# An mLSTM step with the state of a head pair in one block of 128 partitions, GpSimd scaling the old state, and a reciprocal root of one third-order and one Newton step

## The chip, the core and the metric

The kernel runs on one core of a Trainium2 chip. A core has five engines, each with its own queue in program order: TensorE (PE in the profile; its weight loads are a row of their own, PEld), VectorE (DVE), ScalarE (ACT), GpSimd (POOL) and SyncE (SP, which issues DMAs here). PE writes to PSUM, which DVE and ACT read; everything else lies in SBUF. The metric is the device time of one execution in microseconds. The time before is 2581.78 us, the median of three runs between 2577.17 and 2588.86.

## What is computed

One inference step of a two-layer decoder trunk for 1024 new prompt tokens and 8 single-token samples: layer 0 mixes tokens with an mLSTM, layer 1 with multi-head latent attention, and a SwiGLU block follows each. The change lies in the mLSTM of the prompt and in the root that the norms share. The mLSTM runs over chunks of tokens (64 in the reference, 128 in the kernel; the result is the same recurrence). For each head it keeps a matrix state C (64 x 128) and a vector n (64):

```python
def step(carry, xs):
    C, n, m = carry
    ...
    s = jnp.einsum('bhtd,bhsd->bhts', qb, kb) * w_intra
    num = w_inter[..., None] * jnp.einsum('bhtd,bhde->bhte', qb, C) + jnp.einsum('bhts,bhse->bhte', s, vb)
    den = w_inter * jnp.einsum('bhtd,bhd->bht', qb, n) + jnp.sum(s, axis=-1)
    h = num / jnp.maximum(jnp.abs(den), jnp.exp(-m_t))[..., None]
    ...
    C_new = w_C[..., None, None] * C + jnp.einsum('bhs,bhsd,bhse->bhde', w_s, kb, vb)
    n_new = w_C[..., None] * n + jnp.einsum('bhs,bhsd->bhd', w_s, kb)
    return (C_new, n_new, m_new), h
...
h = h * lax.rsqrt(jnp.mean(h * h, axis=-1, keepdims=True) + EPS)
```

Every norm is a root of the form rsqrt(mean + EPS).

## The kernel before

Everything is fp32 in the mLSTM's own products; the large projections are split into a high and a low part and take three products each (`mm3`, L132 to L137). The eight heads lie in two groups of four (hg 0 and 1), and the 1024 tokens in eight chunks c of 128. So `mlstm` (L402) makes 16 steps, i = 2c + hg, in its loop from L500 on. One step is `mlstm_chunk` (L639), in this order:

- E, the weights inside the chunk: DVE (L650) prepares them in the tile Gb, ACT takes the exponential (L651), PE makes k·q on 64 partitions (L656), DVE multiplies (L658).
- kt, the weighted keys (L664), and vn, the values with a column of ones (L666, L670), so that column 128 of a product is the normaliser.
- qw, the queries times the decay (POOL, L677), and wc, the decay at the chunk's end (POOL, L675).
- per pair of heads a PSUM bank: E·vn (L685) and, from chunk 1 on, qw·C added to it (L687). ACT takes |den| (dn, L688) and the sums of squares (ssq, L691).
- kt·vn for the new state (L697), two heads beside each other on 64 columns each, and four DVE operations (L703) that scale the old C and add it. In chunk 0 they are copies (L701).
- the denominators (dn, r: L713, L715), the norm (L716 to L720, with the root of L192) and hn, the normed output (L723, into the tile of E). Its transposes (L727) and the copy to v (L728) belong to the next step.

C is a tile of 128 partitions x 4 heads x 129 columns. A head's state fills only 64 of the partitions, those that its queries lie on in qw; the other 64 stay zero from a memset (L480), so that PE can run over all 128 rows.

The root (L192) makes a first guess with an integer shift and a subtraction (L198, L199) and then three Newton steps of three operations (L201 to L203). It is called once a step on 128 x 4, once for the samples on 128 x 64, six times on up to nine columns (`rms_tok`, L243), and once on 128 x 258 (`rs_of`, L228).

What runs beside a step: in steps 1 to 8 one tile of the output gate's projection (`proj_o`, L465; 72 matmuls of 344 columns) and the samples' own states; in steps 9 to 14 one tile of the output projection of the first 512 tokens (`op_tile`, L885: 24 matmuls of 512 columns, the residual added by DVE into x at L899, the squares summed by POOL at L905), the split of the next weights (wl, L118), and from step 12 on the gating of the other half (L488, L121). The order on each engine comes from a scheduler that works with estimated costs; a few places are fixed by `issue_after`. An engine takes its instructions strictly in that order.

Of the kernel before, what the change touches and what calls it, by code (L numbers as in the profile page):

```python
# [12 lines left out]
AF = mybir.ActivationFunctionType  # L13
ALU = mybir.AluOpType
# [4 lines left out]
P = 128  # L19
# [10 lines left out]
L = 128  # L30
# [61 lines left out]
class Kern:  # L92
# [99 lines left out]
    def rsqrt(self, pool, v, shape, tag, w=None):  # L192
        V = self.nc.vector
        y = self.t(pool, shape, tag + "y")
        u = self.t(pool, shape, tag + "u")
        if w:
            y, u = y[:, :w], u[:, :w]
        V.tensor_scalar(y.bitcast(I32), v.bitcast(I32), 1, None, op0=ALU.logical_shift_right)  # L198
        V.tensor_scalar(y.bitcast(I32), y.bitcast(I32), -1.0, float(0x5F3759DF), op0=ALU.mult, op1=ALU.add)  # L199
        for _ in range(3):  # L200
            V.scalar_tensor_tensor(u, y, -0.5, y, op0=ALU.mult, op1=ALU.mult)  # L201
            V.tensor_tensor(u, u, v, op=ALU.mult)
            V.scalar_tensor_tensor(y, u, 1.5, y, op0=ALU.add, op1=ALU.mult)  # L203
        return y

    def newton(self, y, u, v):
# [120 lines left out]
    def load_x(self):  # L327
# [74 lines left out]
    def mlstm(self, xz, rs, early):  # L402
        nc = self.nc
        w_in = self.mlstm_w_in[0]
        p1 = self.pool("m1")
        v = self.t(p1, [P, 8, T], "v")
# [52 lines left out]
        pi = self.pool("mi")  # L459
# [16 lines left out]

        self.C = []
        for hg in range(2):
            C = self.t(pi, [P, 4, 129], f"C{hg}")
            nc.gpsimd.memset(C, 0.0)  # L480
            self.C.append(C)
        def loaded(og, i, h, zs):
            nc.sync.dma_start(og, o_d[:, h, 512 * i + zs.start:512 * i + zs.stop])
            return og, i, h, zs
# [154 lines left out]
    def mlstm_chunk(self, pi, c, hg, q, k, v, Gb, wb):  # L639
        nc = self.nc  # L640
        V = nc.vector
        s = slice(c * L, (c + 1) * L)
        h4 = slice(hg * 4, hg * 4 + 4)
        j2 = slice(hg * 2, hg * 2 + 2)
# [7 lines left out]
        for hh in range(2):  # L652
            ps = self.mmt("sc")[:, :2 * L]
            for j in range(2):
                r = slice(hh * 64, hh * 64 + 64)
                nc.tensor.matmul(ps[:, j * L:(j + 1) * L], k[r, hg * 2 + j, s], q[r, hg * 2 + j, s], start=True, stop=True)  # L656
            e = E.rearrange("p (j r) t -> p r j t", r=2)[:, hh]
# [3 lines left out]
        ps = self.tp()  # L661
# [5 lines left out]
        ps = self.tp()  # L667
# [3 lines left out]
        C = self.C[hg]  # L671
        qw = None
        if c > 0:
            wc = self.t(pi, [P, 2], "wc", bufs=3)
            nc.gpsimd.tensor_copy(wc, wb[:, :, L - 1])  # L675
            qw = wb
            self.wc = nc.gpsimd.tensor_tensor(qw, q[:, j2, s], wb, op=ALU.mult)  # L677
        dn = self.t(pi, [P, 4], "dn", bufs=2)
        sq = self.t(pi, [P, 4], "ssq", bufs=2)
        banks = []  # L680
        for h0 in (0, 2):
            ps = self.mmt("sc")[:, :258].rearrange("p (j e) -> p j e", e=129)
            for j in range(2):
                h = h0 + j
                nc.tensor.matmul(ps[:, j], E[:, h], vn[:, h], start=True, stop=c == 0)  # L685
                if c > 0:
                    nc.tensor.matmul(ps[:, j], qw[:, h // 2], C[:, h], start=False, stop=True)  # L687
            nc.scalar.activation(dn[:, h0:h0 + 2], ps[:, :, 128], AF.Abs)  # L688
            for j in range(2):
                junk = self.t(pi, [P, L], "junk", bufs=1)  # L690
                nc.scalar.activation(junk, ps[:, j, 0:128], AF.Square, accum_out=sq[:, h0 + j:h0 + j + 1])  # L691
            banks.append((ps, h0))

        ps = self.tp()[:, :258].rearrange("p (j e) -> p j e", e=129)
        for h in range(4):
            r = slice((h % 2) * 64, (h % 2) * 64 + 64)
            nc.tensor.matmul(ps[r, h // 2], kt[:, h], vn[:, h], start=True, stop=True)  # L697
        for h in range(4):
            r = slice((h % 2) * 64, (h % 2) * 64 + 64)
            if c == 0:  # L700
                ins = V.tensor_copy(C[r, h], ps[r, h // 2])  # L701
            else:
                ins = V.scalar_tensor_tensor(C[r, h], C[r, h], wc[r, h // 2:h // 2 + 1], ps[r, h // 2], op0=ALU.mult, op1=ALU.add)  # L703
        self.pin = ins.ins
        if c == NCK - 1:
            for hh in range(2):
                r = slice(hh * 64, hh * 64 + 64)
                Cr = C.rearrange("p (hp hh) e -> p hh hp e", hh=2)[r, hh]
                nc.gpsimd.dma_start(self.C_p[0, 0].rearrange("(hp hh) d e -> hh d hp e", hh=2)[hh, :, j2], Cr[:, :, 0:128])
                with nc.allow_non_contiguous_dma(reason="512 values"):  # L710
                    nc.gpsimd.dma_start(self.n_p[0, 0].rearrange("(hp hh) (d e) -> hh d hp e", hh=2, e=1)[hh, :, j2], Cr[:, :, 128:129])

        V.tensor_tensor(dn, dn, em_t, op=ALU.max)  # L713
        r = self.t(pi, [P, 4], "r", bufs=2)
# [4 lines left out]
        y = self.rsqrt(pi, sq, [P, 4], "f")  # L719
        V.tensor_tensor(y, y, r, op=ALU.mult)  # L720
        hn = E
        for ps, h0 in banks:
            self.hn = V.tensor_tensor(hn[:, h0:h0 + 2], ps[:, :, 0:128], y[:, h0:h0 + 2].unsqueeze(2).to_broadcast([P, 2, L]), op=ALU.mult)  # L723
        yield
        ps = self.tp()
        for j in range(4):
# [1383 lines left out]
```

## Time and profile before

| | |
|---|---|
| median of three runs | 2581.78 us |
| the profiled execution, its own time | 2603.12 us |
| its span | 2601.3 us |
| granted clock of PE, mean | 0.983 |
| mLSTM steps 0 to 15 | about 204 to 455 us of the span |

The profile is of one execution, and its time is its own; it is not one of the three runs. Busy times of engines overlap. PE's rows are pipelined: a row lasts longer than the distance to the next row's start, so distances between starts tell more than lengths. In a row of a timeline stand start, length, engine, line, operation, output<-inputs, shapes and a count, and in brackets how long the engine sat idle and what ended it. In a row of one line's instructions stand the shortest, the median and the longest length in ns.

### The profile page before, as it was taken

To read this page: it belongs to the slowest core of one execution; us is meant where nothing else is said; L and a number is where in the kernel's file an instruction comes from. 1 tells how busy PE (TensorE), PEld (TensorE's weight loads), DVE (VectorE), ACT (ScalarE), POOL (GpSimd) and SP (SyncE) were. 2 spreads that over 40 slices of the span, in tenths; PEclk is the share of its full clock that TensorE was granted. 3 is DMA by queue.
4 is the path that set the end of the run, shared out by engine and by line. 5 is a ranking of instruction groups with operands and counts; after the bars stand their busy time and mean duration, and the time that the engine had idled before them with its cause. 6 is when DMAs were issued, how large, how long until landed. Compare 5 with 4: busy or idle time off the path is not lost.

```text
span 2601.3 us, 54299 instructions
## 1 busy us (share of the span) xinstructions
PE 2510.5 (97%) x21151; PEld 2367.6 (91%) x21151; DVE 1864.6 (72%) x4491; ACT 1328.5 (51%) x3282; POOL 606.3 (23%) x636
## 2 busy tenths in 40 slices
PE   8999999999999999999988889999999999999998
PEld 8999987999999999999976767767899999999998
DVE  4345678897777777666557877768498877777765
ACT  4122344465666666554354555656256656556543
POOL 1021222201111111122335545442211111111102
PEclk9999999999999999999988999999999999999999
DMA  6153554427666566654566676664535566665663
GB/s 196 41 83 95 147 138 106 157 78 149 121 129 124 115 122 128 122 163 150 192 226 247 237 259 225 210 242 147 191 106 113 119 129 127 130 127 115 122 137 113
DMA packets 332087, 382.35 MB, mean 147 GB/s; under 512 B 23433, under 2 KB 263054, under 8 KB 323510
## 3 DMA queue, kind: packets, MB, share of 16 engines
q0 software_dynamic: 60992, 186.65, 31.9%
q1 hardware_dynamic: 258838, 182.04, 23.3%
q10 hardware_dynamic: 12000, 10.20, 1.2%
q8 instruction: 166, 2.72, 0.4%
q14 instruction: 91, 0.75, 0.1%
HBM read 253.37 MB, written 125.44 MB: 146 GB/s over the span
## 4 chain that ended last, share of the span: by engine, by line
PE 69%; DVE 9%; DMA 4%; issue 4%; ACT 2%; POOL 1%; SPq 0%; another core or an unknown queue 0%; POOLq 0%; ACTq 0%; DVEq 0%
PE sc L136 12%; PE sc L134 12%; PE sc L135 12%; PE mm L136 5%; PE mm L135 5%; PE mm L134 5%; PE ss L1892 2%; PE ss L134 2%; PE ss L135 2%; PE ss L136 2%; DMA nat<-in_cache_latent_dram,idx 2%; PE ss L1921 2%; DVE tt L1885 2%; PE mm L1785 1%; DVE wl L118 1%
## 5 line engine op out<-in xcount | busy, mean ns | idle before, releaser
L1215 POOL DMA_DIRECT2D x_d<-wl x72 | 86.8, 1206 | 992.6 <-DVE wl L1214 357.1
L117 ACT ACTIVATE wh<-wr 128x512 fp32r<-128x512 f32 (+2 forms) x167 | 133.4, 799 | 199.7 <-PE mm L135 136.1
L1885 DVE STREAM_TRANSPOSE tt<-nat 128x1024 f32<-128x1024 f32 x128 | 155.4, 1228 | 28.6 <-DMA nat<-in_cache_latent_dram,idx 20.4
L1892 PE MATMUL ss<-tt,qbd 128*32 128x128 f32 x2560 | 101.7, 289 | 18.2 <-issue 8.3
L1892 PEld LDWEIGHTS ss<-tt,qbd 128*32 128x32 f32 x2560 | 76.9, 115 | 40.7 <-issue 17.7
L118 DVE TENSOR_TENSOR wl<-wr,wh 128x1024 fp32r<-128x1024 f32 (+2 forms) x80 | 92.8, 1161 | 28.2 <-ACT wh L117 27.0
L117 ACT ACTIVATE b<-u 128x256 fp32r<-128x256 f32 (+1 forms) x252 | 98.5, 414 | 20.4 <-PE ss L136 6.3
L118 DVE TENSOR_TENSOR b<-u,b 128x256 fp32r<-128x256 f32 (+1 forms) x252 | 103.1, 422 | 6.8 <-ACT b L117 5.4
L1215 POOL DMA_DIRECT2D x_d<-st x72 | 102.4, 1422 | 8.6 <-DVE dC L118 3.5
L134 PE MATMUL mm<-zh,wh 128*128 128x344 f32 x320 | 103.5, 323 | 0.0
L135 PE MATMUL mm<-zl,wh 128*128 128x344 f32 x320 | 103.4, 323 | 0.0
L136 PE MATMUL mm<-zh,wl 128*128 128x344 f32 x320 | 103.3, 323 | 0.0
L118 DVE TENSOR_TENSOR wh<-S,wh 128x512 fp32r<-128x512 f32 x108 | 74.5, 690 | 34.6 <-ACT wh L117 34.3
L117 ACT ACTIVATE wh<-S 128x512 fp32r<-128x512 f32 x108 | 67.9, 629 | 44.4 <-PE sc L136 32.1
L1742 ACT ACTIVATE wr<-sc,mx,rqt 128x512 f32<-128x512 f32 (+2 forms) x96 | 64.6, 676 | 39.5 <-DVE mx L1737 22.8
L134 PE MATMUL sc<-zh,wh 128*128 128x344 f32 x256 | 82.9, 325 | 0.2 <-DVE q L432 0.2
L1785 PE MATMUL mm<-wh,vt 128*128 128x256 f32 (+1 forms) x320 | 74.6, 298 | 8.5 <-ACT wh L117 6.3
L135 PE MATMUL sc<-zl,wh 128*128 128x344 f32 x256 | 82.1, 321 | 0.0
L136 PE MATMUL sc<-zh,wl 128*128 128x344 f32 x256 | 82.0, 320 | 0.0
L1878 POOL DMA_INDIRECT nrp<-in_cache_k_rope_dram,idx x64 | 61.5, 961 | 64.5 <-DVE tt L1885 30.2
L905 POOL TENSOR_TENSOR ss<-ss,sq 128x512 f32<-128x512 f32 (+2 forms) x36 | 51.2, 1423 | 99.4 <-ACT sq L904 99.3
L130 POOL TENSOR_TENSOR wl<-spl,wh 128x512 fp32r<-128x512 f32 x43 | 54.7, 1284 | 83.4 <-ACT spl L129 80.8
(1084 smaller groups left out, 10701.6 us busy)
## 6 DMA issues: line engine op xcount, KB each, us to landing
wr<-in_ffn_w_gate_up_dram SPq DMA_DIRECT2D x96, 512.0 KB
x_d<-st POOLq DMA_DIRECT2D x72, 520.0 KB
x_d<-wl POOLq DMA_DIRECT2D x72, 512.0 KB
dr<-in_ffn_w_down_dram SPq DMA_DIRECT2D x72, 256.0 KB
wr<-in_mlstm_w_in_dram SPq DMA_DIRECT2D x24, 512.0 KB
wr<-in_mlstm_w_out_dram SPq DMA_DIRECT2D x16, 512.0 KB
q<-qn_d SPq DMA_DIRECT2D x28, 256.0 KB
wr<-in_mla_w_o_dram SPq DMA_DIRECT2D x14, 512.0 KB
```

The source lines that it names most:

```text
L117: ins = nc.scalar.activation(hi, src, AF.Copy)
L118: self.low = e.tensor_tensor(lo, src, hi.bitcast(F32), op=ALU.subtract)
L130: nc.gpsimd.tensor_tensor(lo, x, hi.bitcast(F32), op=ALU.subtract)
L134: mm(ps, wh, xh, start=start, stop=False, **kw)
L135: mm(ps, wh, xl, start=False, stop=False, **kw)
L136: self.last = mm(ps, wl, xh, start=False, stop=stop, **kw)
L1215: nc.gpsimd.dma_start(self.x_d[:, 2 * dp:2 * dp + 2, 512 * i:512 * i + 2 * PW[i]], st[i], accum_op=ALU.add)
L1742: nc.scalar.activation(px[:, ks], o, AF.Exp, bias=mx[:, 0:1], scale=f, accum_out=sm[:, c:c + 1])
L1785: nc.tensor.matmul(o, x, y, start=i == 0, stop=i == len(ops) - 1)
L1878: nc.gpsimd.indirect_dma_start(out=nrp[:, s].rearrange("p s c -> p (s c)"), out_offset=None, in_=rop, in_offset=ix)
L1885: V.transpose(out=tt, in_=src.rearrange("p s (c i) -> p c s i", i=32))
L1892: nc.tensor.matmul(psS[32 * j:32 * j + 32, u * P:u * P + P], self.qbd[:, b, cb], tt[:, c, 4 * j:4 * j + 4].rearrange("p s k -> p (s k)"), ...
```

## The change

- C becomes 128 partitions x 2 pairs x 129: the state of an even head lies on partitions 0 to 63, that of the odd head of the same pair on 64 to 127. There are no zeros in it, and no memset.
- qw·C takes only the 64 partitions of its head. The two PSUM banks of a step now hold the even and the odd heads, so both products of a bank take the same half.
- kt·vn already lay in that form, so the new state is one DVE addition of 128 x 258 (a copy in chunk 0). The old state is scaled before by POOL into a new tile Cw (two buffers), which replaces the copy wc.
- The root has one third-order step and one Newton step, seven operations in place of nine behind the first guess.

```diff
-        for _ in range(3):
-            V.scalar_tensor_tensor(u, y, -0.5, y, op0=ALU.mult, op1=ALU.mult)
-            V.tensor_tensor(u, u, v, op=ALU.mult)
-            V.scalar_tensor_tensor(y, u, 1.5, y, op0=ALU.add, op1=ALU.mult)
+        V.tensor_tensor(u, y, y, op=ALU.mult)
+        V.tensor_tensor(u, u, v, op=ALU.mult)
+        V.scalar_tensor_tensor(u, u, -10.0 / 3, u, op0=ALU.add, op1=ALU.mult)
+        V.scalar_tensor_tensor(y, u, 5.0, y, op0=ALU.add, op1=ALU.mult)
+        V.scalar_tensor_tensor(u, y, -0.5 * 0.375 ** 3, y, op0=ALU.mult, op1=ALU.mult)
+        V.tensor_tensor(u, u, v, op=ALU.mult)
+        V.scalar_tensor_tensor(y, u, 1.5 * 0.375, y, op0=ALU.add, op1=ALU.mult)
...
-            C = self.t(pi, [P, 4, 129], f"C{hg}")
-            nc.gpsimd.memset(C, 0.0)
-            self.C.append(C)
+            self.C.append(self.t(pi, [P, 2, 129], f"C{hg}"))
...
-            wc = self.t(pi, [P, 2], "wc", bufs=3)
-            nc.gpsimd.tensor_copy(wc, wb[:, :, L - 1])
+            Cw = self.t(pi, [P, 2, 129], "Cw", bufs=2)
+            nc.gpsimd.tensor_tensor(Cw, C, wb[:, :, L - 1:L].to_broadcast([P, 2, 129]), op=ALU.mult)
             qw = wb
             self.wc = nc.gpsimd.tensor_tensor(qw, q[:, j2, s], wb, op=ALU.mult)
...
-        for h0 in (0, 2):
+        for hh in range(2):
+            r = slice(hh * 64, hh * 64 + 64)
             ps = self.mmt("sc")[:, :258].rearrange("p (j e) -> p j e", e=129)
             for j in range(2):
-                h = h0 + j
+                h = 2 * j + hh
                 nc.tensor.matmul(ps[:, j], E[:, h], vn[:, h], start=True, stop=c == 0)
                 if c > 0:
-                    nc.tensor.matmul(ps[:, j], qw[:, h // 2], C[:, h], start=False, stop=True)
+                    nc.tensor.matmul(ps[:, j], qw[r, j], C[r, j], start=False, stop=True)
...
-        for h in range(4):
-            r = slice((h % 2) * 64, (h % 2) * 64 + 64)
-            if c == 0:
-                ins = V.tensor_copy(C[r, h], ps[r, h // 2])
-            else:
-                ins = V.scalar_tensor_tensor(C[r, h], C[r, h], wc[r, h // 2:h // 2 + 1], ps[r, h // 2], op0=ALU.mult, op1=ALU.add)
+        ins = V.tensor_copy(C, ps) if c == 0 else V.tensor_tensor(C, Cw, ps, op=ALU.add)
...
-        for ps, h0 in banks:
-            self.hn = V.tensor_tensor(hn[:, h0:h0 + 2], ps[:, :, 0:128], y[:, h0:h0 + 2].unsqueeze(2).to_broadcast([P, 2, L]), op=ALU.mult)
+        for hh, ps in enumerate(banks):
+            self.hn = V.tensor_tensor(hn[:, hh::2], ps[:, :, 0:128], y[:, hh::2].unsqueeze(2).to_broadcast([P, 2, L]), op=ALU.mult)
```

Left out are the banks' indices on ACT and the stores of the last state, which follow the new layout.

The scheduler makes a new order from this on DVE and POOL; on PE the order of steps 2 to 8 stays as it was, row for row. In the changed kernel the lines are others: L700 is the sum of C, L709 dn, L719 hn, L895 x, L659 E, L665 kt, L676 Cw, L678 qw.

DVE in the turn from step 11 to step 12, before. fy and fu are the root of step 11, Gb_3915 is E of step 12, Gb_3786 becomes hn of step 11, dn_4084 belongs to step 12:

```order
L899 TENSOR_TENSOR x_3637<-x_3637,mm_4002 128x512
L201 SCALAR_TENSOR_TENSOR fu_3987<-fy_3986 128x4
L118 TENSOR_TENSOR wl_4035<-wr_4032,wh_4034 128x1024
L202 TENSOR_TENSOR fu_3987<-fu_3987,ssq_3950 128x4
L658 TENSOR_TENSOR Gb_3915<-sc_4060,Gb_3915 128x2x128
L203 SCALAR_TENSOR_TENSOR fy_3986<-fu_3987,fy_3986 128x4
L658 TENSOR_TENSOR Gb_3915<-sc_4064,Gb_3915 128x2x128
L720 TENSOR_TENSOR fy_3986<-fy_3986,r_3981 128x4
L664 TENSOR_TENSOR kt_4068<-ss_4069,tok_1126 128x256
L723 TENSOR_TENSOR Gb_3786<-sc_3951,fy_3986 128x256
L723 TENSOR_TENSOR Gb_3786<-sc_3961,fy_3986 128x256
L713 TENSOR_TENSOR dn_4084<-dn_4084,tok_1126 128x4
```

x, wl and E of step 12 stand inside step 11's root, and hn of step 11 lies between kt and dn of step 12. The same turn on DVE after the change (fy_3924 is the root of step 11, Gb_3732 becomes its hn, Gb_3856 is E of step 12):

```order
L206 SCALAR_TENSOR_TENSOR fy_3924<-fu_3925,fy_3924 128x4
L716 TENSOR_TENSOR fy_3924<-fy_3924,r_3919 128x4
L719 TENSOR_TENSOR Gb_3732<-sc_3892,fy_3924 128x2x128
L719 TENSOR_TENSOR Gb_3732<-sc_3902,fy_3924 128x2x128
L895 TENSOR_TENSOR x_3588<-x_3588,mm_3938 128x512
L118 TENSOR_TENSOR wl_3971<-wr_3968,wh_3970 128x1024
L659 TENSOR_TENSOR Gb_3856<-sc_3996,Gb_3856 128x2x128
L659 TENSOR_TENSOR Gb_3856<-sc_4000,Gb_3856 128x2x128
L665 TENSOR_TENSOR kt_4004<-ss_4005,tok_1126 128x256
L709 TENSOR_TENSOR dn_4020<-dn_4020,tok_1126 128x4
L711 RECIPROCAL r_4049<-dn_4020 128x4
L700 TENSOR_TENSOR C_1819<-Cw_4017,ss_4042 128x258
```

The root and hn of step 11 are finished first, then come x, wl, E and kt, and dn follows kt at once. The turns of steps 10 and 12 to 15 have this form too, from step 12 on with the gating between.

POOL in one step of the first part, before (wb is the decay that qw overwrites; s_vb belongs to the samples):

```order
L632 DMA Gb_2576<-G_d_1121 128x4x128
L636 DMA wb_2980<-wi_d_1122 64x2x128 x2
L666 MEMSET vn_3001 128x4
L675 COPY wc_3009<-wb_2779 128x2
L677 TENSOR_TENSOR wb_2779<-q_472,wb_2779 128x256
L833 TENSOR_TENSOR s_vb_2764<-s_vb_2764,s_kw_1933 128x512
```

And after, at the same place (C_1820 is the state of head group 1):

```order
L633 DMA Gb_2554<-G_d_1121 128x4x128
L637 DMA wb_2948<-wi_d_1122 64x2x128 x2
L676 TENSOR_TENSOR Cw_2781<-C_1820,wb_2556 128x258
L667 MEMSET vn_2969 128x4
L678 TENSOR_TENSOR wb_2556<-q_472,wb_2556 128x256
L829 TENSOR_TENSOR s_vb_2737<-s_vb_2737,s_kw_1926 128x512
```

A copy of two columns has become a product of 258 that reads the state, ahead of the memset and of qw, and qw is now that of one step earlier (wb_2556 in place of wb_2779's counterpart), so POOL runs one step less ahead.

More of the change, by code (lines that the diff above doesn't have):

```diff
@@ L680, in mlstm_chunk @@
         banks = []
-        for h0 in (0, 2):
+        for hh in range(2):
+            r = slice(hh * 64, hh * 64 + 64)
             ps = self.mmt("sc")[:, :258].rearrange("p (j e) -> p j e", e=129)
             for j in range(2):
-                h = h0 + j
+                h = 2 * j + hh
                 nc.tensor.matmul(ps[:, j], E[:, h], vn[:, h], start=True, stop=c == 0)
                 if c > 0:
-                    nc.tensor.matmul(ps[:, j], qw[:, h // 2], C[:, h], start=False, stop=True)
-            nc.scalar.activation(dn[:, h0:h0 + 2], ps[:, :, 128], AF.Abs)
+                    nc.tensor.matmul(ps[:, j], qw[r, j], C[r, j], start=False, stop=True)
+            nc.scalar.activation(dn[:, hh::2], ps[:, :, 128], AF.Abs)
             for j in range(2):
                 junk = self.t(pi, [P, L], "junk", bufs=1)
-                nc.scalar.activation(junk, ps[:, j, 0:128], AF.Square, accum_out=sq[:, h0 + j:h0 + j + 1])
-            banks.append((ps, h0))
+                nc.scalar.activation(junk, ps[:, j, 0:128], AF.Square, accum_out=sq[:, 2 * j + hh:2 * j + hh + 1])
+            banks.append(ps)
         ps = self.tp()[:, :258].rearrange("p (j e) -> p j e", e=129)
@@ L707, in mlstm_chunk @@
                 r = slice(hh * 64, hh * 64 + 64)
-                Cr = C.rearrange("p (hp hh) e -> p hh hp e", hh=2)[r, hh]
-                nc.gpsimd.dma_start(self.C_p[0, 0].rearrange("(hp hh) d e -> hh d hp e", hh=2)[hh, :, j2], Cr[:, :, 0:128])
+                nc.gpsimd.dma_start(self.C_p[0, 0].rearrange("(hp hh) d e -> hh d hp e", hh=2)[hh, :, j2], C[r, :, 0:128])
                 with nc.allow_non_contiguous_dma(reason="512 values"):
-                    nc.gpsimd.dma_start(self.n_p[0, 0].rearrange("(hp hh) (d e) -> hh d hp e", hh=2, e=1)[hh, :, j2], Cr[:, :, 128:129])
+                    nc.gpsimd.dma_start(self.n_p[0, 0].rearrange("(hp hh) (d e) -> hh d hp e", hh=2, e=1)[hh, :, j2], C[r, :, 128:129])
         V.tensor_tensor(dn, dn, em_t, op=ALU.max)
```

## The prediction

> **What bounds the kernel now.** I read the page first, then the busy times of the mLSTM loop stage by stage, then the waits and single instructions in it. The change touches that loop (steps 0 to 15, 204 to 455 us of the span) and the reciprocal root that the later norms share.
>
> ```profile
> span 2601.3 us, 54299 instructions
> PE 2510.5 (97%) x21151; PEld 2367.6 (91%) x21151; DVE 1864.6 (72%) x4491; ACT 1328.5 (51%) x3282; POOL 606.3 (23%) x636
> ```
>
> Over the whole span TensorE (PE) is the bound, but an average says little. By stretches (columns: length; busy time and count on PE, PEld, DVE, ACT, POOL; granted clock; DMA):
>
> ```profile
> 241.00:358.00 117.00, 117.00 (x843) 112.22 (x843) 78.61 (x262) 38.76 (x118) 25.98 (x48) 0.99 0.55 138
> 358.00:443.00 85.00, 75.95 (x450) 59.76 (x449) 74.64 (x243) 40.24 (x120) 22.45 (x34) 0.94 0.54 128
> ...
> 258.80:275.62 16.82, 16.82 (x123) 16.11 (x123) 11.14 (x37) 5.70 (x17) 4.01 (x7) 1.00 0.53 134
> ```
>
> Steps 2 to 8 (241 to 358) are PE's: it is never idle, one step is 16.82 us, and VectorE (DVE) has 5.7 us of each free. Steps 9 to 15 (358 to 443) belong to DVE and to the loop DVE, PE, ACT, DVE: DVE is busy 74.64 of 85 us. So DVE work that is saved is worth nothing in the first part, and PE work that is added costs its full length there.
>
> **Part 1: the state product on 64 partitions (steps 2 to 8).** Before, E·v (128 rows of the array) and q·C (128 rows, half of C zero) alternate with equal shape. Afterwards q·C has 64 rows, and the eight products of a step alternate between 128 and 64. The trace has both situations. Every fp32 product is two instructions; this is the timeline of step 5 on PE (start, length):
>
> ```profile
> 289.39 0.47 PE L807 MATMUL ss<-s_qm,s_C 128*128 128x2 f32 x3
> 289.79 0.37 PE L656 MATMUL sc<-q,k 64*128 64x128 f32 x1
> ...
> 290.01 0.51 PE L656 MATMUL sc<-q,k 64*128 64x128 f32 x6
> ...
> 290.23 0.29 PE L656 MATMUL sc<-q,k 64*128 64x128 f32 x2
> 290.44 0.44 PE L663 MATMUL ss<-ct,k 128*128 128x128 f32 x2
> ...
> 292.71 0.39 PE L687 MATMUL sc<-C,wb 128*128 128x129 f32 x2
> 292.94 0.39 PE L685 MATMUL sc<-vn,Gb 128*128 128x129 f32 x2
> ```
>
> Equal shapes follow each other every 0.112 us (292.71 to 292.94 is two). Three L807 end in a start at 289.61 (their rows overlap; 289.39 and two spacings), and the first 64-row product starts 0.18 later, the second of the same rows 0.22 after that: 0.07 and 0.11 over the spacing, 0.18 for the way in. Out of it, 290.23 to 290.44 is 0.21, and the second L663 starts at about 290.61 (0.44 less one length of 0.27), 0.17 later: 0.10 and 0.06 over, 0.16. One switch is therefore about 0.17 us.
>
> A step gains seven switches: 128 to 64 four times, back three times (the last way out goes to L697, whose narrow columns make a switch there already). 7 x 0.17 = 1.17 us a step, and in the seven steps 2 to 8 nothing hides it: **+8.2 us**. Bounds: if only the first wait of each switch is paid (0.07 to 0.10), 7 x 0.09 x 7 = +4.4; if both waits are always the largest (0.10 and 0.11), 7 x 0.21 x 7 = +10.3; zero is a rival below.
>
> The Trainium skill says against this change (TensorEngine Tiling (Array Packing), Key Properties) that changing the tiling mode, not just the tile, drains the TensorE; it gives no price. By that rule the sum is the one above, without it Part 1 would be zero, and the rows just shown agree with the rule.
>
> **Part 2: what DVE saves and what GpSimd takes back.**
>
> ```profile
> L703 DVE SCALAR_TENSOR_TENSOR C<-C,wc,ss x56: 335/348/357, 244.5 to 442.0; 64x129 f32<-64x129 f32 x56
> L658 DVE TENSOR_TENSOR Gb<-sc,Gb x32: 406/416/425, 215.9 to 436.7; 128x256 f32<-128x256 f32 x32
> ...
> 391.08 1.07 DVE L703 SCALAR_TENSOR_TENSOR C<-C,wc,ss 64x129 f32<-64x129 f32 x3
> ...
> 406.27 0.16 DVE L201 SCALAR_TENSOR_TENSOR fu<-fy 128x4 f32<-128x4 f32 x1
> ...
> 406.66 0.16 DVE L203 SCALAR_TENSOR_TENSOR fy<-fu,fy 128x4 f32<-128x4 f32 x1
> ```
>
> Four updates of C at 0.36 apart become one sum of 128x258 out of PSUM, like L658 with 0.42: -1.0 us a step. The root goes from nine small operations to seven; two of them span 0.39 (406.27 to 406.66): -0.39. But GpSimd (POOL) gets a multiplication of 128x258, and its nearest relative, L677 with 128x256, shows what that does to DVE:
>
> ```profile
> 403.58 0.16 DVE L716 TENSOR_TENSOR ssq<-ssq,r 128x4 f32<-128x4 f32 x1
> 403.92 0.71 DVE L717 TENSOR_TENSOR ssq<-ssq,r 128x4 f32<-128x4 f32 x1
> ...
> 403.61 0.19 POOL L675 COPY wc<-wb 128x2 f32<-128x2 f32 x1 [1.39 <-DVE C L703]
> 403.88 0.73 POOL L677 TENSOR_TENSOR wb<-q,wb 128x256 f32<-128x256 f32 x1
> ```
>
> L716 and L717 are the same operation; the one that starts beside POOL's product ends with it, 0.55 us late. The small copy L675, which goes, delayed nothing. The new product waits for the C of two steps earlier, so it starts right behind DVE's sum, where DVE has L650 and L716 next: I charge another 0.55 (bounds: 0 where DVE waits anyway, 0.75 its whole length). Net for DVE: -1.0 - 0.39 + 0.55 = -0.85 us a step. In steps 2 to 8 this vanishes in DVE's 5.7 us of slack.
>
> **Part 3: steps 9 to 15.** Here the order on DVE counts more than its sum. Before, x (L899), wl (L118) and E of the next step stand inside the root; afterwards they stand behind hn, and dn follows kt at once, so the products' latency lies open. Before has that order once, from step 12 to 13:
>
> ```profile
> 362.49 0.15 DVE L713 TENSOR_TENSOR dn<-dn,tok 128x4 f32<-128x4 f32 x1
> ...
> 376.06 0.69 DVE L899 TENSOR_TENSOR x<-x,mm 128x512 f32<-128x512 f32 x1 [2.19 <-PE mm L136]
> ...
> 381.54 0.15 DVE L713 TENSOR_TENSOR dn<-dn,tok 128x4 f32<-128x4 f32 x1
> ...
> 401.63 0.16 DVE L713 TENSOR_TENSOR dn<-dn,tok 128x4 f32<-128x4 f32 x1 [0.94 <-ACT dn L688]
> ...
> 407.99 0.41 DVE L723 TENSOR_TENSOR Gb<-sc,fy 128x256 f32<-128x256 f32 x1
> 408.32 0.68 DVE L899 TENSOR_TENSOR x<-x,mm 128x512 f32<-128x512 f32 x1
> 408.92 1.22 DVE L118 TENSOR_TENSOR wl<-wr,wh 128x1024 fp32r<-128x1024 f32 x1
> 410.05 2.18 DVE L488 SCALAR_TENSOR_TENSOR ot<-ot,v 128x256 f32<-128x256 f32 x3
> 412.16 1.27 DVE L121 SCALAR_TENSOR_TENSOR zh1l<-ot,g,zh1h 128x256 fp32r<-128x256 f32 x3
> 413.35 0.74 DVE L658 TENSOR_TENSOR Gb<-sc,Gb 128x256 f32<-128x256 f32 x2
> ...
> 417.81 0.17 DVE L713 TENSOR_TENSOR dn<-dn,tok 128x4 f32<-128x4 f32 x1 [3.39 <-ACT dn L688]
> ...
> 442.40 0.16 DVE L713 TENSOR_TENSOR dn<-dn,tok 128x4 f32<-128x4 f32 x1
> ...
> 409.81 1.47 POOL L905 TENSOR_TENSOR ss<-ss,sq 128x512 f32<-128x512 f32 x1 [1.56 <-ACT sq L904]
> ```
>
> One loop, from dn to dn: dn to hn is 401.63 to 408.40, 6.77, less 0.85: 5.9. Then x 0.60, wl 1.13, about 1.15 in which POOL's sum of squares (L905, until 411.28) blocks whatever comes next (the L488 of 410.05, whose row of three is 2.18, about 1.0 unblocked), and E's first half 0.34: 3.2. Then the eight products, 8 x 0.224 + 1.17 = 3.0, and 0.4 until ACT has the last |dn| (L697 follows the products at 417.50, in a row further down, and dn starts at 417.81): 3.4. Together 12.5. The five loops from dn of step 10 to that of step 15 make 62.5; gating work (a full set of L488 and L121 is 2.3) in three of them adds about 3.5, and the first, in which two roots interleave, about 1.5: 67.5. Before they took 442.40 - 381.54 = 60.9, so +6.6. I take off 2.9 because dn of step 10 no longer waits behind the root of step 9: the products of step 10 follow the first output tile's matmuls directly. These end when x starts, at 376.06, by my reckoning 1 us earlier after the change, since DVE reaches the operands sooner; 3.4 behind 375.1 is 378.5, and dn was at 381.54. Behind the last dn another 0.5 comes back, since its tail is shorter though x and wl move behind it. **About +3.2 us**; bounds -6 (the 0.85 come through in all seven steps) and +10 (no gain at step 10, every loop 13).
>
> **Part 4: the rest.** Steps 0 and 1 copy C with one instruction in place of four; at the 1.0 of the later steps that is 0 to -2, and since PE had little idle time there I take -0.5. Outside the loop the root runs on few columns six times and once on 258:
>
> ```profile
> L201 DVE SCALAR_TENSOR_TENSOR tu<-ty x18: 155/167/596, 464.1 to 1914.7; 128x4 f32<-128x4 f32 x6, 128x5 f32<-128x5 f32 x6, 128x9 f32<-128x9 f32 x6
> ...
> L201 DVE SCALAR_TENSOR_TENSOR rsu<-rsy x3: 412/422/428, 1215.5 to 1222.7; 128x258 f32<-128x258 f32 x3
> ```
>
> Two operations less each, at most 6 x 0.4 + 2 x 0.43 = 3.3; PE has matmuls beside most of them, so -1 (bounds 0 and -3.3). The two memsets of C that go are no one's wait.
>
> **The sum.** 8.2 + 3.2 - 0.5 - 1 = +9.9 us. On the profiled execution (2603.1 us, the span of 2601.3 and 1.8 around it) that is 2613.0; the median shown, 2581.8, is 21.3 lower, and the same sum gives 2591.7. **Forecast 2592 us**, 0.4% longer.
>
> **Rivals.**
> *The switch costs nothing.* PE would load the 64-row weights beside the running product, as it does between equal shapes. Part 1 is then zero and Part 3 loses 6 x 1.17: 3.2 - 7 = -3.8; with Part 4, -5.3: **2576**. Against it: the waits around L656 above. If DVE's saving also came through in full (-6), 2574.
> The Trainium skill would allow this (TensorE: Matmul & The Clock Gate, step-by-step part of Part 2): weight loads are pulled ahead where row groups don't conflict or where they go to the background buffer. The trace does not bear it out at L656, where the load begins only with the product.
>
> *Slower: the clock falls in steps 10 to 15.* The longer loop leaves PE without work twice a step, before hn and before E; from the lengths of Part 3 I estimate 1.5 to 2 us each. Before the change such a stretch stands here:
>
> ```profile
> 410.00:415.00 5.00, 3.10 (x14) 2.44 (x13) 4.42 (x10) 1.51 (x4) 1.28 (x1) 0.90 0.94 219
> 415.00:420.00 5.00, 5.00 (x29) 4.33 (x28) 1.99 (x8) 1.60 (x10) 0.00 (x0) 0.76 0.26 77
> ...
> 413.90 0.69 PE L685 MATMUL sc<-vn,Gb 128*128 128x129 f32 x2 [1.91 <-DVE Gb L658]
> 417.50 0.66 PE L697 MATMUL ss<-vn,kt 128*64 128x129 f32 x8
> ```
>
> After 1.91 us idle the granted clock fell, and the products took 3.60 in place of 1.8. With the switches stretched as well that is about 2.6 a loop; in four loops +10.4: **2603**. It decides where the idle stretch before E reaches some 2 us in most steps.
> The Trainium skill speaks against it (TensorE: Matmul & The Clock Gate, Part 1): the clock halves only after an idle window of about 3.4 us. The trace has it after 1.91, so I keep the rival.
>
> *The change doesn't do what it says.* POOL now computes qw one step later than before, behind a product that waits for C; if PE had to wait for qw, each step would lose POOL's 0.73 + 0.73, some 20 us in 14 steps: **2612**. But qw is still ready about a step ahead of its use.
>
> **How the numbers follow.** Forecast 0.58, clock 0.25, no switch cost 0.13, late qw 0.04. A measurement of this kernel tells about 0.5% from no change, here 2568.9 to 2594.7. The forecast's own range, 2583 to 2600, lies below that upper bound with two thirds; the no-cost case lies below 2568.9 with a fifth. Slower: a third of 0.58, nearly all of 0.25 and 0.04, together 0.46; faster: 0.03 from the no-cost case and 0.02 from the forecast's own tail, 0.05; same: the rest, 0.49. The range over the cases, with a tenth left out at each end: 2575 to 2605.
>
> **What would show it.** Right: in steps 2 to 8 the step grows from 16.82 to 18.0, with starts 0.18 to 0.22 apart around the 64-row product; C's sum takes 0.42; L716 or L650 behind it takes 0.5 longer beside POOL's product; dn waits 2 to 3 us for ACT in steps 11 to 15. Wrong: a step of 16.8, or steps 9 to 15 shorter than 80 us from first dn to last (362.5 to 442.4 before), in which case DVE's sum counted and not its order.

## The result, and the profile after

The changed kernel takes **2602.5 us** (median of six runs, 2594.0 to 2609.2) where the kernel before takes 2582.0 beside it (six runs, 2576.8 to 2589.1): 1.0075 times as long, 95% interval 1.0057 to 1.0094. A second set of runs, below, gives 1.0066 (1.0052 to 1.0080). So it is slower, by 17 to 20 us, where the forecast was +9.9: inside the range (2575 to 2605) and above the forecast's own (2583 to 2600), on the side that had a chance of 0.46.

The head of the page after, engine by engine:

```profile
span 2600.1 us, 54207 instructions
PE 2512.1 (97%) x21151; PEld 2365.7 (91%) x21151; DVE 1845.9 (71%) x4395; ACT 1329.0 (51%) x3282; POOL 608.3 (23%) x634
```

DVE has 18.7 us less to do and the time grows all the same. This span is shorter than the 2601.3 shown of before, because that execution lay 21 us over the median of its kernel; so a second execution of before serves as the control from here on (the first run below). In both kernels dn starts once a step, so the stretches go from the dn of step 2 to that of step 9, from there to that of step 15, and over one step (length; busy time and count on PE, PEld, DVE, ACT, POOL; granted clock; DMA). The changed kernel:

```profile
244.70:372.36 127.66, 126.71 (x858) 115.71 (x852) 75.71 (x241) 40.07 (x121) 29.62 (x47) 1.00 0.55 131
372.36:453.26 80.90, 75.45 (x405) 56.14 (x406) 61.66 (x191) 37.75 (x107) 24.42 (x33) 0.96 0.49 121
263.02:281.18 18.16, 18.16 (x128) 16.61 (x124) 10.38 (x33) 5.72 (x18) 4.45 (x7) 1.00 0.52 122
```

And the control, the same three:

```profile
244.02:362.46 118.44, 117.45 (x858) 112.22 (x852) 82.31 (x276) 40.03 (x122) 26.02 (x48) 1.00 0.55 140
362.46:440.18 77.72, 69.03 (x421) 54.06 (x418) 69.74 (x228) 37.87 (x110) 21.37 (x32) 0.98 0.53 128
261.00:277.82 16.82, 16.82 (x128) 16.11 (x124) 11.14 (x37) 5.70 (x18) 4.00 (x7) 1.00 0.58 144
```

The changed kernel is 0.7 us behind at the dn of step 2. Between the dn of steps 2 and 9 the change costs 9.2 us, a step 1.34, with the same number of matmuls in it. From step 9 to 15 it costs 3.2, though DVE has 8 us less to do there. Together that is 13.1 us. On PE, a step's eight products read like this (timeline: start, length):

```profile
295.68 0.49 PE L687 MATMUL sc<-vn,Gb 128*128 128x129 f32 x2
296.10 0.49 PE L689 MATMUL sc<-C,wb 64*128 64x129 f32 x2
296.52 0.49 PE L687 MATMUL sc<-vn,Gb 128*128 128x129 f32 x2
...
298.61 0.49 PE L689 MATMUL sc<-C,wb 64*128 64x129 f32 x2
```

A product starts every 0.42 us, where before two instructions took 0.224: each change of rows, whichever way, costs 0.195. On DVE and POOL behind the same step (the sum of C, and what POOL's two products do):

```profile
299.80 0.42 DVE L700 TENSOR_TENSOR C<-Cw,ss 128x258 f32<-128x258 f32 x1
...
300.48 0.80 DVE L713 TENSOR_TENSOR ssq<-ssq,r 128x4 f32<-128x4 f32 x1
300.62 0.63 POOL L676 TENSOR_TENSOR Cw<-C,wb 128x258 f32<-128x258 f32 x1
...
301.33 0.81 POOL L678 TENSOR_TENSOR wb<-q,wb 128x256 f32<-128x256 f32 x1
301.47 0.70 DVE L714 TENSOR_SCALAR ssq<-ssq 128x4 f32<-128x4 f32 x1
```

The one sum takes 0.42 as reckoned. L713 and L714 are two small operations of the norm. L713 ends with the new product and is 0.64 longer than the 0.16 of its kind; L714 ends with qw and is 0.53 longer, as L717 was before.

### The profile page after: what moved, and what is told of

It reads as the page before. It is cut to its first block, busy times and chain, and to the rows that moved or that the text cites. A ratio compares the mean times of both kernels' runs of the same rounds, so it can differ in the third digit from the quotient of the medians.

```text
span 2600.1 us, 54207 instructions
## 1 busy us (share of the span) xinstructions
PE 2512.1 (97%) x21151; PEld 2365.7 (91%) x21151; DVE 1845.9 (71%) x4395; ACT 1329.0 (51%) x3282; POOL 608.3 (23%) x634
## 3 DMA queue, kind: packets, MB, share of 16 engines
q0 software_dynamic: 60992, 186.65, 31.5%
## 4 chain that ended last, share of the span: by engine, by line
PE 71%; DVE 7%; DMA 5%; issue 3%; ACT 2%; POOL 2%; POOLq 0%; ACTq 0%; SPq 0%; DVEq 0%
PE sc L134 13%; PE sc L136 13%; PE sc L135 13%; PE mm L135 6%; PE mm L136 6%; PE mm L134 5%; DMA nat<-in_cache_latent_dram,idx 2%; PE ss L134 2%; PE ss L135 2%; PE ss L136 2%; PE ss L1888 2%; DVE tt L1881 2%; PE ss L1917 1%; PE mm L1781 1%; PE sc L689 1%
## 5 line engine op out<-in xcount | busy, mean ns | idle before, releaser
L1881 DVE STREAM_TRANSPOSE tt<-nat 128x1024 f32<-128x1024 f32 x128 | 155.5, 1229 | 32.3 <-DMA nat<-in_cache_latent_dram,idx 25.6
L1888 PE MATMUL ss<-tt,qbd 128*32 128x128 f32 x2560 | 90.3, 285 | 8.4 <-DVE tt L1881 6.1
L1781 PEld LDWEIGHTS mm<-wh,vt 128*128 128x128 f32 x320 | 56.0, 198 | 20.3 <-ACT wh L117 11.2
```

The source lines that it names most:

```text
L1781: nc.tensor.matmul(o, x, y, start=i == 0, stop=i == len(ops) - 1)
L1881: V.transpose(out=tt, in_=src.rearrange("p s (c i) -> p c s i", i=32))
L1888: nc.tensor.matmul(psS[32 * j:32 * j + 32, u * P:u * P + P], self.qbd[:, b, cb], tt[:, c, 4 * j:4 * j + 4].rearrange("p s k -> p (s k)"), ...
```

## The experiments

Three sets, each on one chip; the kernel before took 2584.4 us on the first and 2597.3 on the second and third, so each kernel is compared with before on its own chip, and an expected time counts by its distance from 2584. Beside the ratios stand, from the trace of one execution each, the time between the dn of two neighbouring steps in steps 3 to 7, the start of the 3001st matmul (behind the mLSTM), and how many windows of 3.41 us of the half clock fell between 200 and 480 us. Before was traced on the first chip (before_again), but not on the other two, so these three columns compare across chips; the changed kernel's step is 18.16 in each of its executions.

| kernel | ratio to before, 95% | a step | matmul 3001 at | half windows |
|---|---|---|---|---|
| before, first execution | | 16.82 | 477.1 | 4 |
| before_again | 1.0007 (0.9991 to 1.0023) | 16.82 | 474.6 | 2 |
| root_alone | 0.9987 (0.9973 to 1.0002) | 16.82 | 470.7 | 1 |
| rows64_alone | 1.0098 (1.0079 to 1.0116) | 18.17 | 499.4 | 8 |
| changed, first execution | 1.0075 (1.0057 to 1.0094) | 18.16 | 487.8 | 2 |
| after_again | 1.0066 (1.0052 to 1.0080) | 18.16 | 492.0 | 5 |
| after_look | one run, 1.0085 | 18.16 | 493.1 | 8 |
| old_root | 1.0099 (1.0080 to 1.0118) | 18.17 | 500.6 | 9 |
| after_stt2 | 1.0077 (1.0050 to 1.0103) | 18.17 | 493.9 | 7 |
| grouped | 0.9982 (0.9967 to 0.9997) | 16.55 | 467.1 | 2 |
| qc_kq | 0.9966 (0.9952 to 0.9979) | 16.35 | 466.7 | 4 |
| qc_kq_stt2 | 0.9970 (0.9956 to 0.9984) | 16.35 | 464.3 | 2 |
| qc_kq_old_root | 0.9979 (0.9966 to 0.9993) | 16.35 | 468.0 | 2 |
| old_root_fill | one run, 1.0093 | 18.17 | 506.3 (its 3193rd: 192 are added) | 2 |

### Where does before usually stand? (before_again)

The kernel before, without an edit.

> The kernel before, unchanged, as a control. The profile shown of it came from an execution of 2603 us, 21 us above the median of its timed runs, so it isn't known where its usual execution stands in each stage. Up to the matmul at 1297.5 us the changed kernel is 10.5 us behind that one execution, yet the medians differ by 20.5 us. Theory A (a slow execution): a usual execution of before passes the same matmul at 1297 us, within 2, and takes 1280 us from there to its end, where the profiled one took 1304 and the changed kernel 1292; then about half of the 20.5 us lies in the attention stage. Theory B (all is in the mLSTM): the usual execution passes that matmul near 1288 us and takes as long from there as the changed kernel does, 1292. Ratio to before 1.000, within 0.002.

It passes the matmul of theory A (the 9501st) at 1293.2, between the two, and needs 1295 us from there, so neither theory holds as it stood. The first execution of before lost 2.5 us in the mLSTM and some 9 in the attention stage against this one, so the pair of traces shown first hid some 11 us of the loss. Against the control the changed kernel is 13.2 us behind at the end of the mLSTM and 14.8 at the 9501st matmul.

### The 64 rows alone (rows64_alone)

```diff
-        for h0 in (0, 2):
+        for hh, r in enumerate((slice(0, 64), slice(64, 128))):
...
-                    nc.tensor.matmul(ps[:, j], qw[:, h // 2], C[:, h], start=False, stop=True)
+                    nc.tensor.matmul(ps[:, j], qw[r, j], C[r, h], start=False, stop=True)
```

> Before, with the product of queries and state alone changed: 64 rows of its head, the banks by even and odd heads; the state stays on 64 partitions of four blocks, its update is the four DVE operations, the root is the old one. Theory of the switch (0.195 us more at each of seven changes between 128 and 64 rows, as the changed kernel's starts show): a step of 16.82 becomes 18.2 in steps 2 to 8 (+9.4 us there), and since nothing is saved on DVE, up to 1.37 more in each of steps 9 to 15: +12 to +18 in all, about 2596. Rival (the step grows because the DVE or GpSimd work was rearranged, the switch is only beside it): a step of 16.8 to 17.0 and 2580 to 2585.

The windows of one step and of steps 9 to 15:

```profile
282.59:300.77 18.18, 18.18 (x128) 16.62 (x124) 11.14 (x37) 5.70 (x18) 3.99 (x7) 1.00 0.54 125
374.55:463.61 89.06, 82.79 (x413) 60.67 (x412) 70.13 (x226) 38.06 (x111) 21.42 (x32) 0.88 0.46 111
```

With DVE's work and order nearly as before, the step is that of the changed kernel. The rival falls. The whole loses 25 us (0.0098 x 2584), more than the whole change does, and more than the 12 to 18 expected: the granted clock in steps 9 to 15 is 0.88 where the control has 0.98. So this one edit is at least as slow as everything together. That the other parts of the change give something back is likely, but the intervals touch.

### The root alone, and the change without it (root_alone, old_root)

In root_alone the kernel before gets the seven operations of the new root, in old_root the changed kernel keeps the nine of the old one; the lines are those of the change's diff.

> Before, with the new root alone. Theory (DVE's savings are hidden or give back little): steps 2 to 8 stay at 16.82 us, steps 9 to 15 move by -3 to +3 as the order on DVE moves, the rest by 0 to -3: 2576 to 2585. Rival (the root's new order or values disturb the later stages, which is where the medians differ by more than the mLSTM): 2590 or more, with the mLSTM as before.

> The changed kernel with the old root of three Newton steps; all else as changed. Theory: steps 2 to 8 at 18.16 us as in the changed kernel, steps 9 to 15 up to 3 us longer by the two operations that come back in each step (0.39 us x 7): 2600 to 2608. Rival (the root is what costs in the later stages): 2590 to 2595, ten below the changed kernel.

root_alone leaves the step at 16.82 and ends the mLSTM 3.9 us earlier; its ratio is 3.4 us of gain with an interval that reaches no change. Its rival falls. old_root loses 25.6 us, a little over the 16 to 24 expected, and its rival falls too. By this the new root is worth 6 to 9 us in the changed kernel (0.0099 less 0.0066 or 0.0075, of 2590), though the intervals overlap or touch. The step is the same. Of the 12.8 us by which old_root's mLSTM ends behind the changed kernel's first execution, 8.8 stand in steps 9 to 15, at a low clock again, and most of the rest ahead of the dn of step 2, where three half windows lie. In those, dn of step 10 to dn of step 15:

```profile
394.20:466.35 72.15, 67.49 (x341) 50.34 (x340) 50.61 (x169) 28.16 (x85) 20.88 (x26) 0.88 0.38 91
```

### The same work in another order (grouped)

```diff
+        pss = [self.mmt("sc")[:, :258].rearrange("p (j e) -> p j e", e=129) for hh in range(2)]
         for hh in range(2):
             for j in range(2):
-                nc.tensor.matmul(ps[:, j], E[:, h], vn[:, h], start=True, stop=c == 0)
-                if c > 0:
-                    nc.tensor.matmul(ps[:, j], qw[r, j], C[r, j], start=False, stop=True)
+                nc.tensor.matmul(pss[hh][:, j], E[:, 2 * j + hh], vn[:, 2 * j + hh], start=j == 0, stop=c == 0 and j == 1)
+        if c > 0:
+            for j in range(2):
+                for hh in range(2):
+                    r = slice(hh * 64, hh * 64 + 64)
+                    nc.tensor.matmul(pss[hh][:, j], qw[r, j], C[r, j], start=False, stop=j == 1)
```

> The changed kernel with the eight products in another order: four of E and v on 128 rows, then four of queries and state on 64 rows, the two halves in turn; same work, same sums. Theory of the switch (0.195 us at each change of rows, nothing for the 64 rows themselves): one change is left of the seven, and two products on different halves run beside each other as k and q do; a step of 16.82 + 0.20 - 0.45 = 16.6 in steps 2 to 8 (17.0 if the halves don't overlap), 8 to 11 us less there than the changed kernel, and at least 1.2 less in each loop of steps 9 to 15: 2580 to 2590 in all. Rival (a product on 64 rows is slow in itself, 1.34/4 = 0.33 us each, whatever stands before it): 18.16 as in the changed kernel, 2600.

The eight products on PE, and the windows of the step and of steps 9 to 15:

```profile
292.15 1.16 PE L685 MATMUL sc<-vn,Gb 128*128 128x129 f32 x8
293.24 0.72 PE L690 MATMUL sc<-C,wb 64*128 64x129 f32 x8
293.89 0.66 PE L702 MATMUL ss<-vn,kt 128*64 128x129 f32 x8
...
277.96:294.51 16.55, 16.55 (x125) 15.73 (x123) 10.27 (x32) 5.67 (x18) 4.40 (x8) 1.00 0.53 142
361.22:432.35 71.13, 64.58 (x405) 49.83 (x406) 60.24 (x191) 36.74 (x107) 23.56 (x33) 0.98 0.56 137
```

The step was expected at 16.6 and takes 16.55. Products on 64 rows are not slow; side by side on the two halves the four take 0.65 us, less than the four on 128. So the step's loss was the changing to and fro and nothing else. Steps 9 to 15 take 9.8 us less than in the changed kernel's first execution. It ends the mLSTM 20.6 us before that execution; by the ratio it gains 4.7 us on before (0.8 to 8.6), where between 4 less and 6 more was expected.

### The products ahead of E (qc_kq)

Cw, qw and the first block below now stand right behind the products of k and q, the second where it was.

```diff
+        if c > 0:
+            for j in range(2):
+                for hh in range(2):
+                    r = slice(hh * 64, hh * 64 + 64)
+                    nc.tensor.matmul(pss[hh][:, j], qw[r, j], C[r, j], start=j == 0, stop=False)
...
+                nc.tensor.matmul(pss[hh][:, j], E[:, 2 * j + hh], vn[:, 2 * j + hh], start=c == 0 and j == 0, stop=j == 1)
```

> The changed kernel with the four products of queries and state moved up, right behind k and q, which have the same 64 rows; E and v are then added to them. No change of rows is left beyond those of the kernel before. Theory of the switch and of the loop: a step of 16.82 - 0.45 = 16.4 in steps 2 to 8 (-3 us against before); in steps 9 to 15 only four products of E and v (0.9 us) stand between E and dn where the changed kernel has eight and seven changes of rows (3.0): loops of 9 to 11 us, no half clock, and the two operations saved in the root count: 2565 to 2577, faster than both. Rival (DVE's order sets the loops, not PE): steps 2 to 8 the same, steps 9 to 15 as long as in the changed kernel: 2585 to 2592.

PE in one step (the projection's matmuls between them left out), and the windows of the step and of steps 9 to 15:

```profile
287.49 0.72 PE L657 MATMUL sc<-q,k 64*128 64x128 f32 x8
288.04 0.62 PE L673 MATMUL sc<-C,wb 64*128 64x129 f32 x8
288.59 0.44 PE L678 MATMUL ss<-ct,k 128*128 128x128 f32 x2
...
290.20 1.16 PE L691 MATMUL sc<-vn,Gb 128*128 128x129 f32 x8
...
275.53:291.88 16.35, 16.35 (x124) 15.68 (x123) 10.06 (x33) 5.68 (x18) 4.86 (x7) 1.00 0.55 141
358.29:431.30 73.01, 65.88 (x400) 51.81 (x400) 61.77 (x191) 36.84 (x103) 23.01 (x31) 0.91 0.55 133
```

16.35 where 16.4 was expected, and steps 9 to 15 take 73.0 in place of 80.9. The gain on before is 0.34% (8.8 us, between 5.5 and 12.5), the lowest ratio of all: it beats both kernels, at the lower end of the 7 to 19 expected. The rival falls. Two things came otherwise. The clock still falls here (0.91): four windows. And steps 9 to 15 are no shorter than grouped's 71.1, in which the four products of queries and state still stand behind E: what moving them ahead of E is worth beyond grouping them is the 0.2 us a step, and no gain shows in these steps or, with overlapping intervals, in the whole.

### What GpSimd's product is worth (after_stt2, qc_kq_stt2)

```diff
-            nc.gpsimd.tensor_tensor(Cw, C, wb[:, :, L - 1:L].to_broadcast([P, 2, 129]), op=ALU.mult)
+            nc.gpsimd.tensor_copy(wc, wb[:, :, L - 1])
...
-        ins = V.tensor_copy(C, ps) if c == 0 else V.tensor_tensor(C, Cw, ps, op=ALU.add)
+        for j in range(2):
+            ins = V.tensor_copy(C[:, j], ps[:, j]) if c == 0 else V.scalar_tensor_tensor(C[:, j], C[:, j], wc[:, j:j + 1], ps[:, j], op0=ALU.mult, op1=ALU.add)
```

> The changed kernel without GpSimd's product: the old state is scaled and added by DVE in two operations of 128 x 129, with the small copy of the decay on GpSimd as before; E, v, queries and state stay in the changed order. It tells what the scaling on GpSimd is worth. Theory (it takes back what it saves: two DVE operations of about 0.36 for one of 0.42, against 0.6 us for which DVE is held beside GpSimd's product): 18.16 us a step in steps 2 to 8, steps 9 to 15 within 4 us of the changed kernel's, 2597 to 2606. Rival (the saving counts): steps 9 to 15 longer by 0.3 x 7 or more with the clock lower: 2605 to 2612. Second rival (GpSimd's product costs more than that, by holding qw back): 2590 to 2596.

> The moved-up products together with the two DVE operations in place of GpSimd's product and the one sum. Theory: steps 2 to 8 as with the products moved up alone, 16.4; steps 9 to 15 within 3 us of it either way, since DVE pays 0.3 more and is held 0.6 less in each step: 2562 to 2580. Rival: with PE's part short, DVE is the bound there, and whichever keeps DVE less time wins by 2 to 4 us.

Neither can be told from the same kernel with the product on GpSimd: 1.0077 beside 1.0066 and 1.0075, 0.9970 beside 0.9966. Which engine scales the old state did not show. The rival of qc_kq_stt2 isn't settled: its mLSTM ends 2.4 us earlier, but with two half windows less.

### The executions, and the root with a short PE part (after_again, after_look, qc_kq_old_root)

> The changed kernel, unchanged, as a control: by the traces the mLSTM costs it 13.2 us against the control of before (10.7 against the first execution shown), by the medians it loses 20.5, 95% between 14.8 and 24.3. Theory A (the execution shown was a mild one): the half clock comes and goes in steps 10 to 15 from one execution to the next, and another execution shows the mLSTM 15 to 20 us behind before, with a lower clock there. Theory B (the mLSTM costs 11 to 13 in each execution, and the rest lies behind it): the mLSTM ends within 1 us of 487.8 as in the first trace. Ratio 1.006 to 1.009 in both.

> The changed kernel once more, for a third look at the same places. Theory A: steps 9 to 15 differ by 1 us or more between its executions, and always where the granted clock differs; steps 2 to 8 take 18.16 in each. Theory B: both the same within 0.5 us.

Theory A holds in size: the mLSTM ends 13.2, 17.5 and 18.5 us behind the control in three executions of one kernel, with 2, 5 and 8 half windows. Its place was wrong: steps 9 to 15 differ by 1.1 us at most (80.9, 81.0, 82.0), and that in after_look, which has three windows more there. Three of after_again's windows lie around the dn of step 2, one of after_look's behind the dn of step 8. A window goes with about 1 us here (4.3 us for three more, 5.3 for six more).

> The products of queries and state moved up behind k and q, with the old root of three Newton steps. In the changed order the old root made the mLSTM 13 us longer, in the kernel before the new root saved 4. Theory (most of the 13 was the clock, which fell because PE sat idle for 2.2 us before E): here PE's part is short, the clock holds, and the old root costs the two operations of DVE alone, 0.39 x 7 and a little more by the order: 2 to 5 us more than with the new root in the mLSTM. Rival (the root's order on DVE is worth 10 us by itself): 10 or more.

0.9979 against 0.9966 is 3.4 us for the old root, with intervals that overlap, and the mLSTM ends 1.3 later with two half windows less, where 2 to 5 was expected. The rival of 10 falls.

### Filling the idle place (old_root_fill)

```diff
+            if c >= 5 and hh == 0:
+                for x in range(16):
+                    nc.tensor.matmul(full[:, 384:512], self.ident, self.ident, start=True, stop=True)
```

> The changed kernel with the old root, whose steps 12 to 15 ran at a granted clock of 0.79 to 0.86, with sixteen products of the unit matrix with itself added ahead of E and v in each of steps 10 to 15: 3.6 us of work for PE in each, in columns that nothing reads, in the place where PE sat idle for 2.2 us; the matmuls of the output tile that stood there move behind the products. Theory of the clock (idle time brings the half clock, and the half clock makes the loop long): granted clock 1.00 in these steps, and dn of step 10 to dn of step 15 takes 62 to 68 us in place of 72.2, though PE has 20 us more to do. Rival (the clock falls for another reason, or costs nothing there): 72 or more, by up to 3.6 in each step.

PE's row before E·v in step 13 of old_root, with the idle time to be filled, and the stretch from dn 10 to dn 15 of old_root_fill:

```profile
430.59 0.46 PE L684 MATMUL sc<-vn,Gb 128*128 128x129 f32 x2 [2.21 <-DVE Gb L656]
```

```profile
392.28:469.58 77.30, 74.31 (x486) 61.39 (x487) 48.29 (x161) 27.34 (x83) 21.35 (x26) 1.00 0.40 86
```

The first half of the theory came as expected: the clock is 1.00 where it was 0.88. But this is one execution, and the number of half windows varies from one execution to the next without an edit. The second half didn't come: 77.3 us, not 62 to 68, a time that the rival named. The filling and the matmuls that it moved stand in the loop themselves; 18 us of work were added in five loops, which grew by 5. What the half clock alone costs there can't be read from this run.

## Why the prediction came out as it did

- **The time as a whole** lies in the range, but its upper end was set by the clock rival (2603). The sum itself, +9.9, is about half of the 17 to 20 measured.
- **Part 1, +8.2: right in kind, a little small.** Measured +1.34 a step and 9.2 us from the dn of step 2 to that of step 9. The term mis-sized was the price of one switch, 0.17, read from L656; here both waits (0.20 into the new shape, 0.214 to its second instruction) are paid at each of the seven, 0.195 over the spacing. Rows64_alone, grouped and qc_kq show it from three sides. The rival without a switch cost is refuted. The Trainium skill (TensorEngine Tiling (Array Packing), Key Properties: a change of the tiling mode drains the engine, different tiles run in parallel) agrees with both: 0.195 for a change, and 0.65 us for four products on two halves.
- **Part 2: right, and worth nothing in steps 2 to 8.** The sum takes 0.42, the hold beside the new product 0.64 (0.55 charged). after_stt2, without that product, shows no difference.
- **Part 3, +3.2: the sum met, partly by luck.** Steps 9 to 15 lost 3.2, 3.3 and 4.3 us in three executions against the control. But the sum was worked out from the first execution of before, and against that one the first execution of the changed kernel lost only 1.0 there (80.9 against 79.9). And the loop from dn of step 11 to that of step 12 is 11.68, not 12.5. Its rows after the change:

```profile
400.68 0.16 DVE L709 TENSOR_TENSOR dn<-dn,tok 128x4 f32<-128x4 f32 x1 [3.10 <-ACT dn L690]
...
406.44 0.68 DVE L895 TENSOR_TENSOR x<-x,mm 128x512 f32<-128x512 f32 x1
407.04 1.22 DVE L118 TENSOR_TENSOR wl<-wr,wh 128x1024 fp32r<-128x1024 f32 x1
407.93 1.46 POOL L901 TENSOR_TENSOR ss<-ss,sq 128x512 f32<-128x512 f32 x1 [0.63 <-ACT sq L900]
408.17 0.75 DVE L659 TENSOR_TENSOR Gb<-sc,Gb 128x256 f32<-128x256 f32 x2
408.74 0.46 PE L687 MATMUL sc<-vn,Gb 128*128 128x129 f32 x2
...
412.36 0.16 DVE L709 TENSOR_TENSOR dn<-dn,tok 128x4 f32<-128x4 f32 x1 [3.10 <-ACT dn L690]
```

  dn to the end of hn takes 5.8 (5.9 charged), and the products, from E to dn, 3.6 (3.4). What failed is the 1.15 for POOL's sum of squares "blocks whatever comes next": L659 starts 0.24 after L901 and runs at its usual length, 0.75 for two. One of its operands lies in PSUM; those of L713 and L714, which were held, all lie in SBUF; that this is the reason was not tried. dn of step 10 came earlier, as reckoned (15.88 behind dn of step 9, before 18.5 and 19.1). The five loops from the dn of step 10 to that of step 15 took 65.0 us, not 67.5. The three with gating work took the 41 charged (40.9), though the 1.15 fell away in them too: something else filled its place. One half window (439.12) lies in these loops; the rest stays open.
- **Part 4, -1.5:** between the 3001st and the 3501st matmul, where the norms' roots lie, the changed kernel gains 0.7 on the control.
- **The rival of the falling clock** (0.25, +10.4 in the loops) was the step that failed: it was taken as one that comes in four loops or not at all. It comes in some executions and not in others, and also around the dn of step 2 and behind that of step 8. The mLSTM costs 13.2 us with no more half windows than the control has, and up to 18.5 with six more, where the sum had 9.9; the rest of 17 to 20 is within the intervals. The condition "decides where the idle stretch before E reaches some 2 us" was too strict:

```profile
423.62 0.49 PE L687 MATMUL sc<-vn,Gb 128*128 128x129 f32 x2 [0.57 <-ACT vn L671]
```

```profile
423.28:426.69 3.41, 3.07 (x15) 2.22 (x16) 2.24 (x5) 1.09 (x6) 0.50 (x1) 1.00 0.90 233
426.69:430.10 3.41, 3.41 (x14) 2.48 (x15) 2.02 (x8) 0.80 (x5) 1.10 (x2) 0.50 0.63 183
430.10:433.52 3.42, 3.42 (x18) 2.76 (x16) 3.11 (x16) 1.11 (x2) 0.43 (x1) 1.00 0.01 1
```

  These are a PE row and three windows of after_look. PE was idle for 0.57 us and then ran the eight products with their seven switches; the next window ran at 0.50. Whether the waits inside the switches count as idleness for the clock was not tried by a run of its own, but the traces speak for it. Between 200 and 480 us, the seven executions without the alternation (both of before, root_alone, grouped and the three qc_kq) fall to the half clock 15 times, always behind a window in which PE's rows fill at most 2.2 of the 3.41 us; none of their 41 windows with 2.2 to 3.1 us of rows stands ahead of a fall. The seven with it (three of the changed kernel, rows64_alone, old_root, after_stt2, old_root_fill) fall 21 times, 11 of them behind such a fuller window (of 33), and once, in after_look, behind a window in which PE was never idle and ran the last products of step 8:

```profile
351.59:355.00 3.41, 3.41 (x26) 2.62 (x25) 1.49 (x4) 1.60 (x10) 0.94 (x2) 1.00 0.76 209
355.00:358.41 3.41, 3.41 (x14) 3.41 (x15) 2.79 (x16) 0.30 (x1) 1.71 (x4) 0.50 0.33 41
```

  So a row's length hides waits that the clock seems to count. The four windows of qc_kq come behind emptier ones (at most 1.56 us of rows).
- **The late qw** (+20) did not come: the step holds no wait for it.

So the loss is the alternation of 128 and 64 rows on PE, first by its own 1.34 us in seven steps where PE bounds, then in the loops of the later steps, and by a clock that falls more often (2 to 9 half windows in the seven executions with it, 1 to 4 in the seven without). The new layout isn't slow in itself: with its products in another order the kernel is 0.2 to 0.3% faster than before.

## What to carry to other kernels

A matmul on half the rows is no slower than one on all, and two on different halves run side by side; but put them next to each other and next to others of that shape, since each change of shape costs here what nearly two instructions of 128 columns cost. Ahead of moving work between DVE and GpSimd, ask which engine bounds the stage: in steps 2 to 8 PE did, and the operations saved on DVE left the step where it was (16.82 with the new root alone). A product that needs no late operand (queries and state) can start its accumulation first, beside others of its shape; that this shortens the wait behind E was expected and did not show.

## What the runs showed of the hardware

The half clock comes in whole windows of 3.41 us on a grid that runs by itself: in the changed kernel's first execution they begin at 377.68 and 439.12, 18 windows apart. In each execution here all falls lie on one such grid. The second of them and its neighbours, and ahead of them PE's row that began in the window before:

```profile
436.11 0.46 PE L687 MATMUL sc<-vn,Gb 128*128 128x129 f32 x2 [1.98 <-DVE Gb L659]
...
435.70:439.12 3.42, 3.01 (x15) 2.19 (x16) 1.32 (x4) 0.88 (x6) 0.00 (x0) 1.00 0.53 154
439.12:442.53 3.41, 3.41 (x14) 2.53 (x15) 1.97 (x11) 0.80 (x5) 0.91 (x2) 0.50 0.15 39
442.53:445.95 3.42, 3.42 (x23) 2.71 (x21) 2.99 (x14) 1.74 (x3) 1.52 (x3) 1.00 0.20 39
```

A gap does not decide by itself: ahead of the products of step 13 PE is idle for 0.56, 0.56 and 0.57 us in the three executions of the changed kernel, and the clock falls behind it in after_look alone. So one and the same gap halves the clock in one execution and not in the next. The Trainium skill (TensorE: Matmul & The Clock Gate, Part 1) has the free-running window, and the trace agrees; that an idle window of about 3.4 us is needed, the trace doesn't bear out: 0.57 us of idle time lay ahead of one fall, 1.98 ahead of another, and in none of the 36 falls counted above was PE idle for the whole window ahead (the emptiest, in root_alone, has 0.73 us of rows).

The sets, each on its own chip, differ most in one place. From the 9751st to the 10001st matmul, in the attention stage, every kernel of the first set takes 23.9 to 24.5 us and every one of the second and third 31.5 to 32.5 (old_root_fill, with its 192 more matmuls, counted from the 9943rd); the first execution of before is of the second kind, with 31.6. There PE waits again and again, "issue" in its rows (nothing that the profile shows ended the wait), as here in that execution:

```profile
1371.32 0.43 PE L1892 MATMUL ss<-tt,qbd 128*32 128x128 f32 x4 [1.00 <-issue]
1372.74 0.43 PE L1892 MATMUL ss<-tt,qbd 128*32 128x128 f32 x4 [0.99 <-issue]
```

The control has no such wait at that place. Why they come was not tried.
